# A decoder layer in one kernel: weight stream, recurrent steps, dense expert blocks and last sums rearranged

## Chip, cores and metric

One core of a Trainium2 chip. The metric is the device time of one execution in microseconds (us). Engines: TensorE (PE), VectorE (DVE), ScalarE (ACT), GpSimd (POOL), SyncE (SP, which issues most DMAs). All times below come from the measured runs or from one profiled execution.

## What is computed

One layer for a prompt of 512 tokens and 8 single sampled tokens, all in float32, width 1024 (520 columns together, since activations lie transposed):

```python
sh1, sc1, g1, sh2, sc2, g2 = split(silu(c) @ w_ada + b_ada, 6)
h = rms_norm(x, norm1_w) * (1 + sc1) + sh1
qa, ka, va, qh, fh, ih, gh, ga, gb = split(h @ w_in)
att = merged attention of 3 dilated windows, 8 heads (samples: over caches)
f = lb + (1 - lb) * sigmoid(fh)        # recurrent branch, 8 heads, 128 x 128 state
o = chunked recurrence with decay f, key 1 - f, value ih, query silu(qh)
hg = rms_norm(o, hg_norm_w) * silu(gh)
x = x + g1 * ((sigmoid(ga) * (att @ w_br_a) + sigmoid(gb) * (hg @ w_br_b)) @ w_o)
h2 = rms_norm(x, norm2_w) * (1 + sc2) + sh2
x = x + g2 * peer_ffn(h2)              # 16 of 16384 experts for each of 8 heads and token
```

`peer_ffn` chooses experts by two sets of 128 keys, and sums gelu(h2 . u) * weight * v over the chosen rows u, v of two tables of 16384 x 1024.

## The kernel before

Each float32 weight tile (128 x 1024, 512 KB, `raw`) is split into a high part (ACT, `whi`, line 132) and a low part (DVE or POOL, `wlo`, line 133), and each product is three matmuls. `raw` has 4 buffers, `whi` and `wlo` 3.

Stages in order of time:
- Front (to 59 us). `mods` multiplies 8 slabs of `w_ada` as they are (two loads each), `norms` the prompt's norm, then `modulate_chunk` and `modulate_samples` write `hT_hi` and `hT_lo`. This part is put in order by the compiler's planner.
- From line 311 to 919 a section with an order written by hand (`manual_schedule`): each engine, SP's queue too, runs its instructions in the order of the text. `plan` lists the weight tiles; `weights_in` (line 339) hands out tile k, having issued loads to k + 3 and splits to k + 2; `product` multiplies it with `hT`.
- Attention (59 to about 530 us): four pairs of heads, each with 9 products (`qkv`). `beside()` runs one step of each open generator ahead of every product: `second_norms`, and `slots`, the attention of the pair before. `slab` multiplies one of the other 16 slabs of `w_ada` (two short tiles); there is one behind each of the first 16 products.
- Recurrent stage (about 530 to 952 us): for each head four products (f, q, v, gg) and a gate. `chain(h)` (line 709) is a generator of ten steps; two heads are open at a time, and a step of each stands ahead of every product. By step: logarithm of f and its running sum `bb` (scan); `kd`, `eb`, decays 0 and 1; transposes of v (`pts`, `vt`), product k q; transposes of kd, pairs 0 and 1, load of the samples' state `ss`; pairs 2; pairs 3; pairs 4 and 5, update of `ss`; pairs 6, new states; output products and `norm_bc`; the rest of the norm (`finish`) and the gate. `decode_attention` is the samples' attention over the caches in 51 steps: POOL multiplies loaded taps, DVE reduces them, and PE sums (`total`, line 665). `step_all` calls it once after each `beside()`, twice in every fourth step.
- Branches, `w_o`, second norm (952 to 1108 us), then the expert queries and their scores (to about 1213 us). The splits `a_hi`, `a_lo`, `g_hi`, `g_lo` of the two branch inputs stand at the start.
- Choices (about 1224 to 1570 us, again ordered by hand from line 975): `choose_tile` picks 16 of 256 sums for one of four tiles of tokens on DVE, in 16 steps. Tile 3 goes by gathers of single rows (`step`, POOL's indirect DMAs and DVE), tiles 0 to 2 dense: for each of 128 blocks of 128 experts all activations are computed (`dense`, line 1091) and weighted by a matrix G, which is built in 48 steps from one-hot products (line 1356), staged by ACT and written to DRAM (`d_G`). `ahead` computes the dense activations of one of the first NSP = 56 blocks early and stores them (`d_ge`): in choose_tile(3) and choose_tile(0) at every third step with POOL's low split, then with DVE's in the 12 of 16 steps that `GU` names, and what is left after the steps.
- Last stage (1614 to 2437 us): for each block `out_block` adds 18 products with v to six PSUM banks; for blocks from NSP on `dense` is computed here, for the others `ge` is loaded again. The gathers go on beside this.
- Tail: the six banks times `g2b` on DVE, plus x on POOL, stored by SP (lines 1524 to 1531), ordered by the planner.

## Time and profile before

| | us |
|---|---|
| median of 3 runs | 2453.06 (2452.21 to 2458.89) |
| the profiled execution | 2453.66 |
| its span, first to last instruction | 2451.9 |

| engine | busy us | share of the span |
|---|---|---|
| PE | 2297.9 | 94% |
| DVE | 1760.3 | 72% |
| ACT | 1155.0 | 47% |
| POOL | 660.6 | 27% |

The profile gives the busy time of each engine, the TensorE clock that was granted (1.00 is the upper of its two levels), and for each instruction how long its engine stood idle before it and which event ended that. In a row of a stage the five busy times are those of PE, its weight loads, DVE, ACT and POOL. A row in order of time is: start, length, engine, line, operation, output<-inputs, shapes, count, and in brackets the idle time before it and what ended that. DMA moved 495 MB, 202 GB/s on the mean. A wait that the profile puts down to "issue" has no event that it shows.

### The profile page before, as it was taken

How to read it: one execution, taken by the hardware profiler on the slowest of the kernel's cores; microseconds unless marked ns; L12 is line 12 of the kernel's file. 1: busy time of each engine (PE TensorE's matmuls, PEld its weight loads, DVE VectorE, ACT ScalarE, POOL GpSimd, SP SyncE). 2: the span in 40 equal slices, each digit the busy share in tenths (PEclk: the TensorE clock that was granted, in tenths of full speed). 3: DMA queues.
4: the chain of work that ended last, by engine and by line, in shares of the span. 5: the costliest groups of instructions: out<-in, count | busy, mean ns of one | idle time of the engine just before them, and what ended most of it. 6: DMA issues, size and time to landing. Idle time of an engine off the chain costs nothing.

```text
span 2451.9 us, 37852 instructions
## 1 busy us (share of the span) xinstructions
PE 2297.9 (94%) x14547; PEld 2118.4 (86%) x14547; DVE 1760.3 (72%) x3156; ACT 1155.0 (47%) x1850; POOL 660.6 (27%) x450
## 2 busy tenths in 40 slices
PE   6899999999888988999978989999999999999997
PEld 3788999989888888989978989988888888888886
DVE  3677566548766665547998897477888878788876
ACT  3556566445444443243337778633333333333332
POOL 1110121102221223004450001034444445454433
PEclk9998999999899999999998999989999999999999
DMA  6453212234442324423344555779999999999996
GB/s 220 155 167 113 81 55 70 64 121 141 138 140 90 115 97 157 157 94 96 96 135 168 195 209 199 265 275 331 343 351 328 365 323 344 345 348 331 347 309 206
DMA packets 197466, 495.49 MB, mean 202 GB/s; under 512 B 18123, under 2 KB 84651, under 8 KB 195749
## 3 DMA queue, kind: packets, MB, share of 16 engines
q1 hardware_dynamic: 147636, 313.02, 38.0%
q0 software_dynamic: 39456, 143.28, 16.3%
q10 hardware_dynamic: 10192, 36.77, 4.0%
q8 instruction: 114, 1.87, 0.3%
q14 instruction: 68, 0.55, 0.1%
HBM read 439.17 MB, written 54.49 MB: 201 GB/s over the span
## 4 chain that ended last, share of the span: by engine, by line
PE 43%; DVE 7%; ACT 3%; DMA 1%; issue 1%; ACTq 0%; POOL 0%; POOLq 0%; DVEq 0%; SPq 0%
PE acc L1471 21%; PE ph L1091 16%; PE pp L180 3%; PE pp L1356 2%; ACT oa L1348 1%; DVE wlo L133 1%; ACT whi L132 1%; DVE e L1151 1%; ACT stage L1363 1%; DVE y L1121 1%; DVE sel L1153 0%; PE pt L1177 0%; DMA vr<-in_peer_v 0%; DVE oa L1342 0%; DVE e L1148 0%
## 5 line engine op out<-in xcount | busy, mean ns | idle before, releaser
L133 DVE TENSOR_TENSOR wlo<-raw,whi 128x1024 fp32r<-128x1024 f32 (+1 forms) x254 | 320.0, 1265 | 176.4 <-ACT whi L132 175.2
L1245 POOL DMA_INDIRECT gat<-in_peer_u,idx x128 | 212.6, 1661 | 628.1 <-DVE junk L1272 442.2
L1091 PE MATMUL ph<-h_hi,whi 128*128 128x384 f32 x1024 | 356.4, 348 | 13.4 <-ACT whi L132 13.4
L1091 PE MATMUL ph<-h_hi,wlo 128*128 128x384 f32 x1024 | 351.8, 344 | 8.4 <-POOL wlo L133 7.3
L1091 PE MATMUL ph<-h_lo,whi 128*128 128x384 f32 x1024 | 350.7, 342 | 0.0
L132 ACT ACTIVATE whi<-raw 128x1024 fp32r<-128x1024 f32 (+1 forms) x284 | 292.8, 1036 | 111.3 <-PE pp L180 58.9
L180 PE MATMUL pp<-hT_hi,whi 128*128 128x260 f32 x1344 | 287.9, 297 | 17.2 <-ACT whi L132 17.1
L180 PE MATMUL pp<-hT_hi,wlo 128*128 128x260 f32 x1344 | 280.0, 291 | 5.1 <-DVE wlo L133 5.1
L180 PE MATMUL pp<-hT_lo,whi 128*128 128x260 f32 x1344 | 279.7, 291 | 0.0
L180 PEld LDWEIGHTS pp<-hT_hi,whi 128*128 128x128 f32 x1344 | 218.7, 199 | 20.3 <-ACT whi L132 18.6
L180 PEld LDWEIGHTS pp<-hT_hi,wlo 128*128 128x128 f32 x1344 | 216.6, 197 | 6.9 <-DVE wlo L133 6.9
L180 PEld LDWEIGHTS pp<-hT_lo,whi 128*128 128x128 f32 x1344 | 217.5, 198 | 0.0
L1091 PEld LDWEIGHTS ph<-h_hi,whi 128*128 128x128 f32 x1024 | 197.4, 193 | 17.8 <-ACT whi L132 14.9
L1091 PEld LDWEIGHTS ph<-h_hi,wlo 128*128 128x128 f32 x1024 | 197.0, 192 | 10.4 <-POOL wlo L133 7.9
L1091 PEld LDWEIGHTS ph<-h_lo,whi 128*128 128x128 f32 x1024 | 197.1, 192 | 2.8
L1471 PE MATMUL acc<-vhi,chi 128*128 128x512 f32 x768 | 195.8, 390 | 0.0
L1471 PE MATMUL acc<-vhi,clo 128*128 128x512 f32 x768 | 195.0, 389 | 0.0
L1471 PE MATMUL acc<-vlo,chi 128*128 128x512 f32 x768 | 194.9, 389 | 0.0
L133 DVE TENSOR_TENSOR vlo<-vr,vhi 128x1024 fp32r<-128x1024 f32 x128 | 156.3, 1221 | 52.7 <-ACT vhi L132 52.7
L132 ACT ACTIVATE vhi<-vr 128x1024 fp32r<-128x1024 f32 x128 | 135.3, 1057 | 114.6 <-PE acc L1471 114.6
L1095 ACT ACTIVATE ge<-ph 128x384 f32<-128x384 f32 x128 | 62.6, 489 | 264.9 <-PE ph L1091 264.5
L1245 POOL DMA_INDIRECT gat<-in_peer_v,idx x128 | 162.7, 1271 | 70.9 <-issue 34.0
(378 smaller groups left out, 4531.9 us busy)
## 6 DMA issues: line engine op xcount, KB each, us to landing
raw<-in_uT SPq DMA_DIRECT2D x128, 512.0 KB
vr<-in_peer_v SPq DMA_DIRECT2D x128, 512.0 KB
raw<-in_w_in SPq DMA_DIRECT2D x84, 512.0 KB
raw<-in_w_ada SPq DMA_DIRECT2D x48, 512.0 KB
d_G<-stage ACTq DMA_DIRECT2D x12, 2048.0 KB
gt<-d_G SPq DMA_DIRECT2D x32, 768.0 KB
d_ge<-ge ACTq DMA_DIRECT2D x56, 192.0 KB
ge<-d_ge SPq DMA_DIRECT2D x56, 192.0 KB
```

What stands on the lines that cost most here:

```text
L132: act.activation(hi, src, AF.Copy)
L133: return (eng or dve).tensor_tensor(out=lo, in0=src, in1=hi.bitcast(F32), op=ALU.subtract)
L180: pe.matmul(ps[:, s, :NH], w[:, k, :], x[:, k, s * NH:(s + 1) * NH], start=first and n == 0, stop=last and n == 2)
L1091: pe.matmul(ph[:, :NB], w[:, k], x[:, k, :NB], start=k == 0 and n == 0, stop=k == KC - 1 and n == 2)
L1095: act.activation(ge, ph[:, :NB], AF.Gelu_apprx_tanh)
L1121: dve.match_replace(out=y[:n], in_to_replace=vals[:, 0:8], in_values=x, imm_value=-3.0e38)
L1151: dve.tensor_tensor(out=e3[:n], in0=e3[:n], in1=pb[:n, :, None, :].to_broadcast([n, H, 16, 16]), op=ALU.mult)
L1245: pool.indirect_dma_start(out=t, out_offset=None, in_=A[tab][0], in_offset=bass.IndirectOffsetOnAxis(ap=idx, axis=0))
L1348: act.activation(oas[g][:, j], oas[g][:, j], AF.Copy, scale=sels[t][:, 0, n + j:n + j + 1])
L1356: pe.matmul(pgs[g // 2][:, g % 2, j * P:(j + 1) * P], oa[:, j], ob[:, j], start=True, stop=True)
L1363: act.activation(st[:, :, n0:n0 + 8], pgs.pop(b).rearrange("p s (n i) -> p i (s n)", i=P), AF.Copy)
L1471: pe.matmul(acc[2 * t + d], a[:, t * P:(t + 1) * P], b[:, d * 512:(d + 1) * 512], start=first and n == 0, stop=last and n == 2)
```

## The change

The functions for the plan of tiles move ahead of the front, and `weights_in` is divided into `fetch` and itself; `fetch(0)` is called in the front behind the third slab's columns. The 16 slabs stand behind every other product of the first 32. In `chain`, the scan moves one step later, the transposes of v from the third to the fourth step (in front of the pairs) with kd's behind the pairs, the broadcast load `vb` a step later, and the update of `ss` from the seventh step to the end of the eighth. `finish` runs its matmuls and its square root and returns the other two instructions, which `product` runs after the next tile's loads and splits. The samples' attention gets two calls in every third step. `a_lo` is split on DVE alone. NSP is 60: `ahead` is called in every second step of the two choices, and in 11 of 16 steps of the G loop. In the tail DVE makes three of the six additions, and three of the stores go out by ACT's queue.

```diff
-NSP = 56
+NSP = 60
-GU = (0, 1, 2, 4, 5, 6, 8, 9, 10, 12, 13, 14)
+GU = (0, 1, 3, 4, 6, 7, 9, 10, 12, 13, 15)
 ...
+    def with_slab(hp, n):
+        return (9 * hp + n) % 2 == 0 and 9 * hp + n < 32
 ...
-            if hp == 0 or hp == 1 and n < 7:
-                plan += slab_plan(8 + 9 * hp + n)
+            if with_slab(hp, n):
+                plan += slab_plan(8 + (9 * hp + n) // 2)
 ...
+    def fetch(k):
+        while at_[0] < min(len(plan), k + 4):
+            src, kc = plan[at_[0]]
+            parts[at_[0]] = wtile("raw", F32, RAW)
+            dma.dma_start(parts[at_[0]].rearrange("p (k c) -> p k c", k=kc), src)
+            at_[0] += 1
+        while at_[1] < min(len(plan), k + 3):
+            hi, lo = wtile("whi", F32R, 3), wtile("wlo", F32R, 3)
+            split(hi, lo, parts[at_[1]])
 ...
         for s in mods((0, 4, 1, 5, 2, 6, 3, 7), st, small):
             if s == 0:
                 norms()
+            if s == 1:
+                fetch(0)
 ...
     def product():
-        return proj(None, KC, hT_hi, hT_lo, None, weights_in())
+        w = weights_in()
+        end()
+        return proj(None, KC, hT_hi, hT_lo, None, w)
 ...
             act.activation(two(rs), half(ps), AF.Sqrt, bias=eps)
-            dve.reciprocal(rs, rs)
-            dve.scalar_tensor_tensor(out=x, in0=x, scalar=w, in1=rs, op0=ALU.mult, op1=ALU.mult)
+            def rest():
+                dve.reciprocal(rs, rs)
+                dve.scalar_tensor_tensor(out=x, in0=x, scalar=w, in1=rs, op0=ALU.mult, op1=ALU.mult)
+            return rest
 ...
             bb = t2("bb")
+            yield
             dve.tensor_tensor_scan(bb, reset, lf, 0.0, op0=ALU.mult, op1=ALU.add)
-            yield
 ...
-            pts = bank("pts")
-            pe.transpose(out=pts[:NS, :P], in_=v[:, NT:], identity=ident)
-            vs = hp_.tile([NS, P], F32, tag="vs", name="vs")
-            act.activation(vs, pts[:NS, :P], AF.Copy)
-            after(lambda: dma2.dma_start(d_hv[h], vs))
-            vt = rows(v, "vt")
 ...
             yield
-            kt = rows(kd, "kt")
+            pts = bank("pts")
+            pe.transpose(out=pts[:NS, :P], in_=v[:, NT:], identity=ident)
+            vs = hp_.tile([NS, P], F32, tag="vs", name="vs")
+            act.activation(vs, pts[:NS, :P], AF.Copy)
+            after(lambda: dma2.dma_start(d_hv[h], vs))
+            vt = rows(v, "vt")
             placed = [pairs(0), pairs(1)]
             sides(2)
             decays(3)
             for x in placed:
                 x()
+            kt = rows(kd, "kt")
 ...
             neighbours()
-            for b in range(NS):
-                dve.scalar_tensor_tensor(out=ss[:, b], in0=vb[:, b], scalar=k[:, NT + b:NT + b + 1], in1=ss[:, b],
-                                         op0=ALU.mult, op1=ALU.add)
 ...
                 states.append(new)
+            for b in range(NS):
+                dve.scalar_tensor_tensor(out=ss[:, b], in0=vb[:, b], scalar=k[:, NT + b:NT + b + 1], in1=ss[:, b],
+                                         op0=ALU.mult, op1=ALU.add)
 ...
-            finish()
-            dve.tensor_mul(hg[:, h], ob, d["gg"])
+            rest = finish()
+            def gated():
+                rest()
+                dve.tensor_mul(hg[:, h], ob, d["gg"])
+            ends.append(gated)
 ...
-            for _ in range(2 if late_steps[0] % 4 == 0 else 1):
+            for _ in range(2 if late_steps[0] % 3 == 0 else 1):
 ...
-        split(a_hi[:, c], a_lo[:, c], att[:, c], pool if c % 2 else dve)
+        split(a_hi[:, c], a_lo[:, c], att[:, c], dve)
 ...
     for k, _ in enumerate(choose_tile(3, sel3)):
-        if k % 3 == 0:
+        if k % 2 == 0:
             ahead(pool)
 ...
     for k, _ in enumerate(choose_tile(0, sel)):
-        if k % 3 == 0:
+        if k % 2 == 0:
             ahead(pool)
 ...
             dve.tensor_mul(y, acc[2 * t + d], g2b[:, cols_])
-            pool.tensor_tensor(out=y, in0=y, in1=xo[t][:, cols_], op=ALU.add)
-            dma.dma_start(O["y_prompt"][t][:, cols_], y)
+            ys.append((y, xo[t][:, cols_], O["y_prompt"][t][:, cols_]))
+    for i in (5, 0, 4, 1, 3, 2):
+        y, x, out = ys[i]
+        (dve if i > 2 else pool).tensor_tensor(out=y, in0=y, in1=x, op=ALU.add)
+        (dma if i > 2 else nc.scalar).dma_start(out, y)
```

## Rows read from the trace of the kernel before

**Rows 1.** Stages: from:to, length, busy us (instructions), granted clock, DMA share, GB/s.

```profile
0.00:59.20 59.20, 39.53 (x177) 18.65 (x177) 20.44 (x48) 19.39 (x36) 6.71 (x13) 0.92 0.63 220
59.20:350.00 290.80, 278.75 (x2025) 249.54 (x2026) 202.38 (x274) 176.01 (x245) 39.50 (x27) 0.96 0.36 118
...
500.00:960.00 460.00, 405.27 (x3140) 394.73 (x3140) 299.73 (x545) 221.51 (x347) 93.83 (x67) 0.92 0.39 128
...
1190.00:1290.40 100.40, 82.61 (x499) 80.86 (x497) 95.13 (x348) 34.47 (x45) 54.14 (x25) 0.94 0.43 130
1290.40:1570.20 279.80, 260.22 (x1667) 256.43 (x1668) 228.55 (x457) 223.52 (x518) 14.63 (x10) 0.96 0.57 196
1570.20:1613.60 43.40, 35.47 (x167) 33.81 (x167) 11.59 (x12) 12.93 (x17) 0.00 (x0) 0.84 0.67 238
1613.60:2436.80 823.20, 819.91 (x3986) 728.32 (x3984) 667.20 (x852) 299.19 (x401) 376.11 (x259) 1.00 0.94 332
2436.80:2451.90 15.10, 1.90 (x5) 0.28 (x4) 6.78 (x7) 1.17 (x2) 9.16 (x6) 0.67 0.42 150
```

**Rows 2.** Front: instructions in order of time, a stretch, sizes of loads.

```profile
59.18 0.80 PE L180 MATMUL pp<-hT_hi,whi 128*128 128x260 f32 x2 [14.51 <-ACT whi L132]
...
48.51 1.24 DVE L133 TENSOR_TENSOR hT_lo<-hs,hT_hi 128x64 fp32r<-128x64 f32 x1
...
50.73 0.43 SPq L347 DMA_DIRECT2D raw<-in_w_in  x1
...
15.00:20.00 5.00, 5.00 (x22) 3.51 (x21) 0.00 (x0) 3.47 (x6) 0.00 (x0) 1.00 1.03 411
...
raw<-in_w_in SPq DMA_DIRECT2D x84, 512.0 KB
```

**Rows 3.** Who ended PE's waits from 500 to 960: total, times, longest.

```profile
PE pts L783 <- ACT v L434: 26.4, 7, 5.4
PE pp L180 <- ACT a_hi L132: 7.7, 1, 7.7
PE pl L761 <- DVE w L740: 7.4, 8, 1.9
PE ptm L788 <- issue: 5.6, 1, 5.6
PE pl L761 <- DVE w L746: 3.6, 3, 2.7
```

**Rows 4.** One head's start in order of time, ACT and DVE.

```profile
664.22 0.63 ACT L721 ACTIVATE kd<-kd 128x512 f32<-128x512 f32 x1 [7.42 <-DVE kd L720]
...
667.26 0.58 ACT L434 ACTIVATE v<-pp 128x520 f32<-128x520 f32 x1
...
653.96 1.22 DVE L715 TENSOR_TENSOR_SCAN bb<-reset,lf 128x512 f32<-128x512 bf16 x1 [4.31 <-ACT lf L713]
...
660.31 2.17 DVE L836 SCALAR_TENSOR_TENSOR ss<-vb,k,ss 128x128 f32<-128x128 f32 x8
```

**Rows 5.** A dense block in the chain that ended last; size of a reload.

```profile
1622.02 4.21 PE ph L1091 x24
...
ge<-d_ge SPq DMA_DIRECT2D x56, 192.0 KB
```

**Rows 6.** Who ended PE's waits from 1290.4 to 1570.2.

```profile
PE pp L1356 <- ACT oa L1348: 18.7, 14, 3.0
```

**Rows 7.** First choices in order of time, POOL and DVE.

```profile
1238.68 9.85 POOL L133 TENSOR_TENSOR wlo<-raw,whi 128x1024 fp32r<-128x1024 f32 x3 [7.73 <-ACT whi L132]
...
1246.19 2.42 DVE L1141 TENSOR_SCALAR pp<-pos 128x128 uint32<-128x128 uint32 x1
1248.53 0.21 DVE L1142 TENSOR_SCALAR pp<-pos 128x128 uint32<-128x128 uint32 x1
```

**Rows 8.** Samples' attention in order of time: POOL's addition, PE's sum.

```profile
912.77 1.28 POOL L674 TENSOR_TENSOR tap<-tap 67x512 f32<-67x512 f32 x1
...
925.58 1.00 PE L665 MATMUL pav<-one_v,tap 128*128 128x1 f32 x8
```

More of the change, by code (lines that the diff above doesn't have):

```diff
@@ L241, in layer, with wcol, acol, hcol @@
     hT_lo = fp.tile([P, KC, N], F32R, name="hT_lo")
+    def wcol(c0):
+        return A["w_in"][c0 // P]
+    def acol(t, g, hp):
+        return wcol(t * 1536 + g * 512 + hp * P)
+    def hcol(i, h):
+        return wcol(4608 + i * D + h * P)
+    def gcol(i):
+        return wcol(8704 + i % 2 * D + i // 2 * P)
+    FIRST = ((0, 0), (1, 0), (0, 1), (1, 1), (0, 2), (1, 2), (2, 0), (2, 1), (2, 2))
+    plan = []
+    def with_slab(hp, n):
+        return (9 * hp + n) % 2 == 0 and 9 * hp + n < 32
+    def slab_plan(s):
+        return [(A["w_ada"][s, k2], 4) for k2 in (1, 0)]
+    for hp in range(4):
+        for n, (t, g) in enumerate(FIRST):
+            plan.append((acol(t, g, hp), KC))
+            if with_slab(hp, n):
+                plan += slab_plan(8 + (9 * hp + n) // 2)
+    plan += [(hcol(i, 0), KC) for i in (1, 0, 2, 3)] + [(gcol(i), KC) for i in range(G0)]
+    for h in range(8):
+        plan += [(hcol(i, h + 1), KC) for i in (1, 0, 2, 3)] if h < 7 else []
+        plan += [(gcol(i), KC) for i in GT[h]]
+    parts, at_ = {}, [0, 0, 0]
+    def fetch(k):
[7 more added lines that the diff above has]
+            split(hi, lo, parts[at_[1]])
+            parts[at_[1]] = [x.rearrange("p (k c) -> p k c", k=plan[at_[1]][1]) for x in (hi, lo)]
+            at_[1] += 1
+    def weights_in():
+        k = at_[2]
+        at_[2] += 1
+        fetch(k)
+        return parts.pop(k)
     with tc.tile_pool(name="st", bufs=1) as st:
@@ L312, in layer, with end @@
     flow.__enter__()
-    def acol(t, g, hp):
-        return wcol(t * 1536 + g * 512 + hp * P)
-    def hcol(i, h):
-        return wcol(4608 + i * D + h * P)
-    def gcol(i):
-        return wcol(8704 + i % 2 * D + i // 2 * P)
-    FIRST = ((0, 0), (1, 0), (0, 1), (1, 1), (0, 2), (1, 2), (2, 0), (2, 1), (2, 2))
-    plan = []
-    def slab_plan(s):
-        return [(A["w_ada"][s, k2], 4) for k2 in (1, 0)]
-    for hp in range(4):
-        for n, (t, g) in enumerate(FIRST):
-            plan.append((acol(t, g, hp), KC))
-            if hp == 0 or hp == 1 and n < 7:
-                plan += slab_plan(8 + 9 * hp + n)
-    plan += [(hcol(i, 0), KC) for i in (1, 0, 2, 3)] + [(gcol(i), KC) for i in range(G0)]
-    for h in range(8):
-        plan += [(hcol(i, h + 1), KC) for i in (1, 0, 2, 3)] if h < 7 else []
-        plan += [(gcol(i), KC) for i in GT[h]]
-    parts, at_ = {}, [0, 0, 0]
-    def weights_in():
-        k = at_[2]
-        at_[2] += 1
-        while at_[0] < min(len(plan), k + 4):
-            src, kc = plan[at_[0]]
-            parts[at_[0]] = wtile("raw", F32, RAW)
-            dma.dma_start(parts[at_[0]].rearrange("p (k c) -> p k c", k=kc), src)
-            at_[0] += 1
-        while at_[1] < min(len(plan), k + 3):
-            hi, lo = wtile("whi", F32R, 3), wtile("wlo", F32R, 3)
-            split(hi, lo, parts[at_[1]])
-            parts[at_[1]] = [x.rearrange("p (k c) -> p k c", k=plan[at_[1]][1]) for x in (hi, lo)]
-            at_[1] += 1
-        return parts.pop(k)
+    ends = []
+    def end():
+        while ends:
+            ends.pop(0)()
     def product():
-        return proj(None, KC, hT_hi, hT_lo, None, weights_in())
+        w = weights_in()
+        end()
+        return proj(None, KC, hT_hi, hT_lo, None, w)
     late = []
@@ L566, in second_norms @@
             for n in range(6):
[L567 removed]
+                norms_.pop((hp, n))()()
                 yield
@@ L589, in layer @@
                     under = None
-                if hp == 0 or hp == 1 and n < 7:
+                if with_slab(hp, n):
                     under = slab()
@@ L857, in chain @@
                 states.append(new)
+            for b in range(NS):
+                dve.scalar_tensor_tensor(out=ss[:, b], in0=vb[:, b], scalar=k[:, NT + b:NT + b + 1], in1=ss[:, b],
+                                         op0=ALU.mult, op1=ALU.add)
+            after(lambda: dma2.dma_start(O["hgrn_s"][h], ss))
             after(lambda: dma2.dma_start(O["hgrn_p"][h], states[3]))
@@ L898, in layer @@
             step_all()
+            end()
         begin()
@@ L1524, in layer @@
     xo = [x_rows(d_x[t], P) for t in range(3)]
+    ys = []
     for t in range(3):
```

6 lines of the change are left out of this document (1 added, 5 removed).

## Prediction

> **What bounds the kernel now.** I read the table of stages first: busy time of each engine, granted TensorE clock and DMA share in stretches cut where the work changes. TensorE (PE) is busy in 820 of 823 us of the last stage, 279 of 291 in the attention, and idle for 54.7 us of the recurrent stage, 17.8 of the first choices, 19.6 beside the one-hot products, 7.9 in the stretch after them, 19.7 in the front and 13.2 in the tail [rows 1]. No other engine is full in any stage but VectorE (DVE) with 95 of 100 us in the first choices [rows 1]. So PE sets the time, its instructions are the same after the change, and a gain can come from two places only: PE's idle time, 148 us in the eight rows together, and the time that it works at the lower of its clock levels. The granted clock is a mean of 1.2 and 2.4 GHz; 0.92 over 460 us of the recurrent stage is 0.08 x 460 x 2 = 74 us at the lower level, 0.84 over 43.4 us after the one-hots is 14 us, and it follows the idle stretches (1.00 in the last stage, which has hardly any) [rows 1]. Then I read who ended PE's waits in each stage, and then single waits in order of time.
>
> **Front.** PE stands for 14.51 us until 59.18, for the first part of the first weight tile; that tile's load was issued at 50.73, because it comes behind the front in the order. The last operand of the product, the samples' low part of hT, is done at 48.51 + 1.24 = 49.75 [rows 2]. With four loads issued and three tiles split at the third slab, PE waits for hT instead, and starts 59.18 - 49.75 = 9.4 us earlier. The low clock after the pause, which now partly runs out while PE stands, moves behind the restart; I take off 1.4 for it: -8. The cost that could show: the four loads are 2.1 MB, 5.1 us at the 411 GB/s of 15 to 20 us, a stretch in which DMA is already full [rows 2]. If SP sends them ahead of the last slabs' loads, those come up to 5 us late. The splits add 3 ACT and 3 DVE instructions of about 1.1 and 1.2 us in a part where DVE is busy 20 of 59 us [rows 1]; if the planner, which orders this part, puts them among the last modulations, they cost up to their sum on DVE, 3.7. Bounds -2 and -11.
>
> **Slabs and attention.** The 16 slabs, now behind the first 16 products, go behind every other one of 32. PE's work and DMA bytes are equal. PE is idle for 12.0 us in the 291 us of this stage [rows 1], nearly all of it in the first nine products, where a slab's two short parts leave too little time to split the next tile and no attention steps stand between. Nine such places become five: -12.0 x 4/9 is -5; some comes back where slabs now meet attention steps: -3.5, bounds 0 and -6.
>
> **Recurrent steps.** Here lies most of the gain. Waits of PE in this stage: 26.4 us in 7 places for the copy of v (transposes `pts` of a head's third step), 7.4 and 3.6 for decay products of DVE, 5.6 at the stage's start, 7.7 at its end [rows 3], which leaves 4.0 of the 54.7 in small ones. One wait read in time: ACT's copy of v, at 667.26, is behind the exponentials of kd, and those waited 7.42 us for DVE's kd; DVE had itself stood 4.31 us for ACT's logarithm at the scan and then spent 2.17 us on the state updates of the samples before it came to kd [rows 4]. The change touches each link: the scan goes one step later (no stop of DVE), the state updates go behind the new states, and the transposes of v one step later, a whole product after v. So the 26.4 go. The 3.6 and about 5 of the 7.4, which come behind the reciprocal and the state updates, go with the delayed `rest`. What stays: 5.6 + 4.0 + 2.4. What is late next: first, the products with the samples' states one step after the updates, which now come after DVE's new states; by the one head that I followed, PE arrives about 1 us early. Second, five PSUM tiles in one step where three were, out of four banks, so the fifth waits for ACT's copy of the one before, another 1 us. That is 8 x 2 = 16 us of new waits. The queues that the moved instructions pass: SP's store and broadcast load of v go one step later and are read one step later too; DVE's work in a head is the same. Waits fall from 47.0 to about 28: -19. The low clock: of 74 us I expect 16 fewer while PE works, at half speed: -8. Term -27. Bounds: all waits and half of the low clock gone but the 5.6 and 4.0, -42; every removed wait formed again but a fifth, -8.
>
> **Attention of the samples, branches.** Two calls in every third step instead of every fourth: of 52 calls needed, 41 steps gave 51, now 39 steps give 52, so the sums are done two steps before the end and a_hi can be split before the last gate. The 7.7 us for a_hi [rows 3] shrink, but the last head's norm still ends last for the second product: -5, bounds 0 and -8. Moving two a_lo splits from POOL to DVE is hidden there.
>
> **Four more blocks beside the choices.** One dense block is 24 products in 4.21 us, and leaves the last stage: 4 x 4.21 = -16.8 there [rows 5]. The moves: 8 instead of 6 blocks in each of the two first choices, 33 instead of 36 among the one-hots, 8 instead of 5 after them.
> First choices: DVE sets their length, PE has 17.8 us of idle time and gets 16.8 us of work. About 13 fit, the rest delays nothing since the stage ends with DVE. Cost 0, with 4 us either way.
> Beside the one-hots: PE loses 3 x 4.21 = 12.6 us. Its waits there, 18.7 us in 14 places for ACT's weighing [rows 6], come in steps without a block; these are now 15 instead of 12, so 3 x 18.7/14 = 4 comes back: -8.6.
> After them: 12.6 us more, into 7.9 us of PE's idle time [rows 1] of which about half is filled, and 14 us of low clock of which 6 go at half price: +12.6 - 4 - 3 = +5.6.
> Last stage: its DMA share is 0.94 at 332 GB/s, 273 MB [rows 1]. Four weight tiles (512 KB) become reloads of 192 KB [rows 2, 5], so 272 MB go in 806 us: 337 GB/s. I take +1 for that.
> Sum 0 - 8.6 + 5.6 - 16.8 + 1 = -18.8; bounds +2 (DVE slowed by POOL's splits, DMA holding the last stage) and -26.
> POOL makes the splits of the first choices. Three of them took 9.85 us beside DVE's wide products, and a DVE instruction on 128 x 128 elements took 2.42 us, the next of its kind 0.21 [rows 7]. The Trainium skill's GPSIMD Engine Reference (Specifications) says that the two engines share their SBUF interfaces and contend when DVE reads two tensors from SBUF; the trace agrees. By that rule alone each added split could cost DVE 2.2 us, an estimate of 8.8 for four, and the sum would be -10 in place of -18.8. I stay at 0 because only every second of these calls falls into the wide products, as before.
>
> **Tail.** POOL's six additions fill 9.2 of the last 15.1 us [rows 1]; three of them take half, and DVE gets three more behind its own work: -2, bounds +1 and -4.
>
> **Sum.** -8 - 3.5 - 27 - 5 - 18.8 - 2 = -64. The profiled execution took 2453.66 (span 2451.9), the median of three runs is 2453.06, so the same difference applies: 2389.
>
> **Rivals.**
> B: the waits of the recurrent steps form again, at the samples' states and the banks, at some 5 us per head; the term there is -4 in place of -27, so 2412. For it: DVE is busy 300 of 460 us there and serial with ACT; against: its stops for the logarithm are gone.
> C: DMA becomes the bound of the last stage. If 332 GB/s is what it can move, 272 MB take 819 us instead of 806, and the time is 2402. For it: share 0.94; against: PE waits for nothing there, and 411 GB/s ran in the front [rows 2]. The Trainium skill's page DMA: Bandwidth & Descriptors (Specifications) gives about 358 GB/s of HBM as a core's limit; by it the margin is 6%, by the 411, which differ from it, 18%.
> D: the change does not do what it says in the front: the planner leaves loads or splits behind the modulations. The term is 0, so 2397.
> E, slower: the quicker calls of the samples' attention. PE's sums over the taps wait in PE's order for POOL's additions, and all products stand behind them. POOL ended one at 914.05, PE read it at 925.58, 11.5 us later [rows 8]. Steps get shorter and double calls more frequent; if the margin turns negative, PE stands. At 10 us for each of the eight sums this is +80: -64 + 80 = +16, so 2469. It decides from a tap that lands more than 11 us later relative to PE's step. Against: POOL is busy 94 of 460 us [rows 1].
>
> **How the numbers follow.** Forecast 2389 (own range 2364 to 2410) 0.62, B 0.17, C 0.11, D 0.06, E 0.04. Leaving out E, the upper part of B and the ends of the forecast gives 2355 to 2424 for eight in ten. A measurement of this kernel can tell 0.3%, 7 us, from no change. All cases but E lie below 2446: faster 0.94; same 0.02 (many bounds at their poor ends together); slower 0.04.
>
> **What would show it.** Right: PE's first weight product near 50; no wait at the transposes of v; idle time of the recurrent stage near 30 and its clock near 0.95; 4 fewer blocks in the last stage, which is near 806 us and still without PE waits. Wrong: new waits at the samples' states or the taps' sums; ACT's splits in the last stage waiting for loads; first choices longer than 104 us.

## The result and the profile after

The changed kernel takes 2412.11 us (median of four runs, 2408.19 to 2421.14) against 2452.64 beside it: a ratio of 0.9832, 95% interval 0.9809 to 0.9855, well clear of the 0.3% that a measurement can tell. The forecast was 2389, its own range 2364 to 2410, the whole range 2355 to 2424. So the direction and the range held, and over a third of the forecast gain did not come. The sum hides more than it shows: three terms gained more than forecast, and two, both around other work that PE was to be filled with, are far off on the other side.

The profiled execution took 2409.3 us, its span 2407.5. The engines on its page, beside the table of before:

```profile
PE 2287.8 (95%) x14547; PEld 2109.0 (88%) x14547; DVE 1764.6 (73%) x3157; ACT 1154.5 (48%) x1850; POOL 653.4 (27%) x449
```

To find where the time went, I cut both spans at the same eight events: first product with a streamed weight tile, first product k q of the recurrent stage, first product with `a_hi`, first and last one-hot product, first and last product of `vhi` and `chi` into the six sums, end. The columns are those of [rows 1]. Before, cut so:

```profile
0.00:59.18 59.18, 39.51 (x177) 18.63 (x177) 20.42 (x48) 19.39 (x36) 6.71 (x13) 0.92 0.63 220
59.18:530.20 471.02, 458.97 (x3353) 413.81 (x3354) 301.21 (x455) 267.03 (x376) 61.58 (x41) 0.97 0.30 98
530.20:959.28 429.08, 374.36 (x2907) 366.38 (x2905) 287.25 (x515) 211.16 (x331) 93.52 (x65) 0.91 0.40 132
959.28:1298.60 339.32, 314.43 (x2319) 307.27 (x2319) 243.90 (x830) 123.00 (x177) 100.02 (x59) 0.96 0.38 120
1298.60:1569.70 271.10, 252.87 (x1637) 249.40 (x1638) 221.94 (x442) 220.67 (x513) 13.31 (x8) 0.97 0.56 193
1569.70:1613.70 44.00, 36.07 (x172) 34.41 (x172) 11.59 (x12) 13.43 (x18) 0.23 (x1) 0.84 0.67 239
1613.70:2433.80 820.10, 816.82 (x3973) 725.99 (x3972) 665.78 (x850) 299.19 (x401) 375.92 (x258) 1.00 0.94 332
2433.80:2451.90 18.10, 4.90 (x18) 2.51 (x16) 8.20 (x9) 1.17 (x2) 9.34 (x6) 0.72 0.51 185
```

The changed kernel, cut at the same events:

```profile
0.00:51.66 51.66, 40.73 (x178) 19.12 (x178) 22.06 (x43) 19.38 (x34) 6.75 (x12) 1.00 0.67 247
51.66:535.30 483.64, 465.85 (x3348) 419.87 (x3348) 300.41 (x459) 266.87 (x377) 61.50 (x42) 0.95 0.31 96
535.30:928.71 393.41, 357.53 (x2912) 352.14 (x2910) 292.71 (x516) 209.04 (x330) 90.04 (x66) 0.95 0.45 144
928.71:1270.00 341.29, 327.51 (x2415) 321.76 (x2415) 247.10 (x833) 129.97 (x186) 103.89 (x61) 0.97 0.40 128
1270.00:1534.70 264.70, 241.63 (x1541) 236.71 (x1542) 215.79 (x435) 215.10 (x505) 10.78 (x7) 0.97 0.53 185
1534.70:1592.40 57.70, 51.01 (x267) 49.20 (x267) 17.63 (x18) 19.45 (x26) 0.94 (x1) 0.94 0.66 238
1592.40:2393.50 801.10, 798.68 (x3877) 707.66 (x3877) 660.50 (x846) 293.49 (x393) 375.82 (x258) 1.00 0.95 339
2393.50:2407.50 14.00, 4.92 (x18) 2.53 (x16) 8.43 (x12) 1.17 (x2) 3.71 (x3) 0.85 0.67 244
```

The difference of each length, beside the term of the prediction:

| stage | forecast us | measured us |
|---|---|---|
| front | -8 | -7.5 |
| slabs and attention | -3.5 | **+12.6** |
| recurrent steps, with the wait for `a_hi` | -27 - 5 | -35.7 (the wait itself: +0.2) |
| branches to first choices | 0 | +2.0 |
| one-hot loop | -8.6 | -6.4 |
| after the loop | +5.6 | **+13.7** |
| last stage | -15.8 | -19.0 |
| tail | -2 | -4.1 |
| sum | -64 | -44.4 |

In the front PE now waits for hT, as forecast (instructions in order of time, the ones that answer to [rows 2]):

```profile
51.37 0.24 ACT L132 ACTIVATE hT_hi<-hs 128x64 fp32r<-128x64 f32 x1
51.64 1.28 DVE L133 TENSOR_TENSOR hT_lo<-hs,hT_hi 128x64 fp32r<-128x64 f32 x1
51.66 0.58 PE L180 MATMUL pp<-hT_hi,whi 128*128 128x260 f32 x1 [3.83 <-ACT hT_hi L132]
```

In the recurrent stage the wait of 26.4 us for v [rows 3] is gone. What ended PE's waits there (total, times, longest):

```profile
PE pc L662 <- DVE sc L656: 9.1, 1, 9.1
PE pl L782 <- DVE w L761: 9.0, 7, 2.2
PE pp L180 <- ACT a_hi L132: 7.9, 1, 7.9
PE pl L779 <- DMA tap<-in_cache_kv_w: 5.2, 1, 5.2
```

The first line is new: 9.1 us in a single place, at the transposes of the samples' scores. The decay products of the second line have not got quicker (L782 here is L761 of before: 9.0 us for 7.4 [rows 3]); those of L746 no longer wait. The last line stands near the stage's start, where 5.6 us stood before. Beside the one-hots the wait for ACT's weighing [rows 6] has grown from 18.7 us in 14 places:

```profile
PE pp L1383 <- ACT oa L1375: 24.0, 20, 3.2
```

### The profile page after: what moved, and what is told of

Same layout as the page of the kernel before. It is cut to its first block, busy times and chain, and to the rows that moved or that the text cites. A ratio compares the mean times of both kernels' runs of the same rounds, so it can differ in the third digit from the quotient of the medians.

```text
span 2407.5 us, 37833 instructions
## 1 busy us (share of the span) xinstructions
PE 2287.8 (95%) x14547; PEld 2109.0 (88%) x14547; DVE 1764.6 (73%) x3157; ACT 1154.5 (48%) x1850; POOL 653.4 (27%) x449
## 4 chain that ended last, share of the span: by engine, by line
PE 42%; DVE 8%; ACT 4%; issue 2%; DMA 1%; ACTq 0%; SPq 0%; POOLq 0%; DVEq 0%
PE acc L1498 21%; PE ph L1118 16%; PE pp L180 3%; PE pp L1383 2%; ACT oa L1375 1%; DMA gt<-d_G 1%; DVE wlo L133 1%; ACT whi L132 1%; DVE e L1178 1%; DVE oa L1369 1%; DVE sel L1180 1%; DVE y L1148 1%; ACT stage L1390 1%; PE pt L1204 0%; DVE e L1175 0%
## 5 line engine op out<-in xcount | busy, mean ns | idle before, releaser
L132 ACT ACTIVATE whi<-raw 128x1024 fp32r<-128x1024 f32 (+1 forms) x284 | 292.8, 1037 | 104.6 <-PE pp L180 60.0
L180 PE MATMUL pp<-hT_hi,whi 128*128 128x260 f32 x1344 | 288.3, 297 | 6.3 <-ACT hT_hi L132 4.9
L180 PE MATMUL pp<-hT_hi,wlo 128*128 128x260 f32 x1344 | 279.7, 291 | 1.6 <-DVE wlo L133 1.6
L180 PE MATMUL pp<-hT_lo,whi 128*128 128x260 f32 x1344 | 280.7, 292 | 0.5 <-DVE hT_lo L133 0.5
L180 PEld LDWEIGHTS pp<-hT_hi,whi 128*128 128x128 f32 x1344 | 218.2, 199 | 8.7 <-ACT hT_hi L132 5.1
L180 PEld LDWEIGHTS pp<-hT_lo,whi 128*128 128x128 f32 x1344 | 218.4, 198 | 0.8 <-DVE hT_lo L133 0.8
L180 PEld LDWEIGHTS pp<-hT_hi,wlo 128*128 128x128 f32 x1344 | 216.6, 197 | 2.2 <-DVE wlo L133 2.2
L132 ACT ACTIVATE vhi<-vr 128x1024 fp32r<-128x1024 f32 x128 | 135.3, 1057 | 113.6 <-PE acc L1498 105.4
L1272 POOL DMA_INDIRECT gat<-in_peer_v,idx x128 | 157.6, 1231 | 75.1 <-issue 35.3
```

Source lines behind the costliest of these rows:

```text
L132: act.activation(hi, src, AF.Copy)
L180: pe.matmul(ps[:, s, :NH], w[:, k, :], x[:, k, s * NH:(s + 1) * NH], start=first and n == 0, stop=last and n == 2)
L1272: pool.indirect_dma_start(out=t, out_offset=None, in_=A[tab][0], in_offset=bass.IndirectOffsetOnAxis(ap=idx, axis=0))
```

## The experiments

Each edit starts from the changed kernel, or where it says so from the kernel before. Lengths of stages come from one profiled execution of each, cut at the events above. A difference of less than 7 us (0.3%) between two medians cannot be told from nothing. A stage's length moves too where nothing in it was edited: the attention took 466.5 to 472.2 us in the four kernels that have its old code and the old front, the recurrent stage 392.5 to 396.5 us in the six that have its new code untouched. A difference of some 5 us in one stage of one execution is therefore a hint and not a result.

**Attention: where the slabs stand.** The stage should have gained 3.5 us and lost 12.6. PE waits there for the low half of a slab's second tile:

```profile
PE pm L421 <- DVE wlo L133: 10.7, 10, 2.0
```

That is 10.7 us in all, in 10 places, 2.0 the longest. (The expectations below say 22.7 for it, which is too much: I had added up the columns.) One of the places in order of time, DVE and PE: a reciprocal of a norm and a product stand on DVE ahead of three splits, and the slab's second half waits for the first of these.

```profile
75.46 3.40 DVE L404 RECIPROCAL rs<-rs 128x520 f32<-128x520 f32 x1 [3.74 <-ACT rs L401]
78.90 0.76 DVE L405 SCALAR_TENSOR_TENSOR x<-x,wq,rs 128x520 f32<-128x520 f32 x1
79.57 4.61 DVE L133 TENSOR_TENSOR wlo<-raw,whi 128x1024 fp32r<-128x1024 f32 x3
...
80.85 0.29 PE L421 MATMUL pm<-wlo,c 128*10 128x256 f32 x1 [2.05 <-DVE wlo L133]
```

That was the theory: VectorE comes late. Three kernels tested it.

```
slabs_first16:  with_slab(hp, n): 9 * hp + n < 16
slabs_on_pool:  split(hi, lo, parts[at_[1]], pool if plan[at_[1]][1] == 4 else dve)
slabs_late16:   with_slab(hp, n): 19 <= 9 * hp + n < 35
```

> The changed kernel (2412.1) with the 16 slabs of the attention back behind the first 16 products; nothing else is undone. Theory (the spread slabs meet attention steps, so that VectorE comes late to the low half of a slab's second tile, which TensorE then waits for, and the clock falls more often): the waits of the slabs' products for wlo at their second part go from about 22.7 us back to about 4, the stage from the first product to the end of the attention goes from 483.6 us to about 470, and the time is 2399, between 2396 and 2403. Rival (the stage grew because the stream of weights starts earlier and the same work now stands ahead of it, or because of the delayed second part of the norms): the stage stays at 480 to 484 us and the time at 2409 to 2415.

Measured: 2397.53 us (ratio to before 0.9767, 0.975 to 0.9784), the time that the theory gave. The stage:

```profile
51.31:525.10 473.79, 458.51 (x3347) 413.73 (x3347) 300.21 (x459) 266.82 (x377) 64.09 (x42) 0.97 0.31 98
```

9.8 us shorter than 483.64. The waits for a slab's low half are 6.3 us here, in 5 places, for 10.7 in 10; the theory had 4. Of the 9.8 us 2.5 are PE's idle time (483.64 - 465.85 = 17.8, here 15.3) and 7.3 busy time, with the same instructions at a mean clock of 0.97 in place of 0.95. So the place of the slabs is the cause, but the larger part of the loss is no wait.

> The changed kernel with its spread slabs, where GpSimd in place of VectorE makes the low halves of the slabs' tiles (32 instructions, about 3.3 us each by the split of the first choices, in a stage in which GpSimd is nearly idle). Theory (VectorE's order is what holds the slabs up): the waits for the slabs' wlo shrink from 22.7 us to under 10, though not to nothing, since GpSimd's split takes longer than VectorE's 1.2 us, and the time is 2400 to 2406. Rival 1 (it is not who splits but that a slab's two short tiles leave no time for the splits behind them): the waits stay near 23 us or grow by 2 us for each slab, and the time is 2412 to 2440. Rival 2 (GpSimd slows VectorE's wide instructions beside it): VectorE's attention instructions get longer by some tenths and the stage by 5 us or more.

Measured: 2410.45 us (0.982, 0.9795 to 0.9844), no different from the changed kernel. The stage, and its waits for slabs:

```profile
56.31:536.60 480.29, 466.52 (x3348) 421.20 (x3348) 264.37 (x429) 266.40 (x377) 127.69 (x72) 0.95 0.31 97
```

```profile
PE pm L421 <- POOL wlo L133: 4.1, 2, 2.1
```

The waits fell from 10.7 to 4.1 us, the stage got 3.3 us shorter, and the clock stayed at 0.95; the first product came 4.7 us later (56.31 for 51.66), which ate the rest. VectorE's lateness is thus about a quarter of the 12.6 us, not the main thing. Rival 2 did not happen: VectorE's other instructions in the stage took 212.9 us together, 212.5 in the changed kernel. GpSimd's split took 2.40 us on the mean of 30, not the 3.3 I had assumed.

> The changed kernel with the same 16 slabs behind products 20 to 35, so that every one of them stands beside attention steps (in the changed kernel 11 of 16, with slabs behind the first 16 products 8). Theory (a slab and an attention step together make a long stretch of short matmuls between two products, after which the clock falls; the DVE wait for wlo is not the main part, since GpSimd's splits took most of it away and the time stayed): although the first products get rid of their slabs, the time at the lower clock in the attention rises from 48 us to 60 or more, the stage takes 486 to 495 us in place of 483.6, and the time is 2415 to 2424. Rival (it is the spreading over every other product that costs, with twice as many turns from tiles of 1024 to pairs of short tiles): dense again as in the kernel before, the stage takes 470 to 478 us and the time is 2399 to 2407.

Measured: 2396.27 us (0.9764, 0.9746 to 0.9782). My theory had moved to "a slab beside an attention step costs", and it fell; the rival stands. All 16 slabs stand beside attention steps here (behind the first 16 products it is 7 of them, not the 8 of the expectation), and the stage is 9.4 us shorter:

```profile
51.60:525.80 474.20, 461.71 (x3348) 416.06 (x3348) 300.08 (x459) 266.96 (x377) 61.70 (x42) 0.96 0.32 98
```

```profile
PE pm L421 <- DVE wlo L133: 10.2, 9, 1.5
```

It even keeps 10.2 us of waits for slabs. What costs is that slabs stand behind every other product: behind consecutive products, early or late, they cost about 10 us less, partly in small waits (12.5 to 15.3 us idle in place of 17.8), partly in the clock. Why the clock falls more often in the alternating order these runs do not settle.

**Recurrent steps.** First the new order alone, in the kernel before:

```
 kernel before + chain(h), rest and end() of the changed kernel
 (slabs, fetch, NSP, calls of decode_attention, tail as before)
```

> The kernel before (2452.6) with only the new order of the recurrent steps: the scan and the transposes of v one step later, the update of the samples' state behind the new states, the second part of the norm behind the next tile's splits. Slabs, start of the stream, blocks, calls of the samples' attention and tail are those of before. Theory (this order alone took the 36 us that the stage lost in the changed kernel): the stage takes 385 to 390 us in place of 422, the time is 2413 to 2420, TensorE's waits for the copy of v are gone, and the 9.1 us wait at the transposes of the scores, which I put down to the quicker calls, is not there. Rival (the earlier start, the slabs or the calls have a share in it): the stage takes 395 us or more and the time is over 2424.

Measured: 2415.08 us (0.9837, 0.982 to 0.9855). The stage up to the product with `a_hi`:

```profile
531.50:920.90 389.40, 363.08 (x2913) 357.79 (x2911) 284.60 (x516) 209.66 (x331) 93.38 (x66) 0.93 0.45 146
```

429.08 became 389.40: -39.7, more than the 35.7 in the changed kernel. Without the wait for `a_hi` that is 381.7, a little under the theory's 385 to 390. The wait at the scores is 2.8 us in 2 places here. So the new order alone gives all of the stage's gain. The changed kernel has 9.6 us more of PE's idle time there (35.9 for 26.3) and 5.6 us less busy time; that the quicker calls of the samples' attention cost the idle time is likely, since the wait at the scores is longer with them, but no run undid them alone, and the 4.0 us in length are no more than such a stage moves by itself.

```
 kernel before: only pts, vs, vt moved behind the step that holds pl and decays(2), kt behind the pairs,
 the load of vb a step later
```

> The kernel before (2452.6) with one move out of the recurrent order: the transposes of v one step later, in the place of kd's, and the load that depends on them a step later; scan, update of the samples' state and norm as before. It tells how much of the 39.7 us (the new order alone took these from the stage) hangs on this wait. Theory (the 26.4 us of waiting for v are the main loss and its copy is late only by that one step): the 26.4 us are gone, the other waits stay as they are, and with their share of the low clock the time is 2420 to 2428. Rival (VectorE's stop at the logarithm and the early update of the samples' state keep ScalarE late, so that TensorE meets the next operand, the decay products, late instead): the waits for v shrink, those at the pairs grow, and the time is 2433 or more.

Measured: 2427.67 us (0.9901, 0.9882 to 0.992), the theory at its upper edge. Stage and waits:

```profile
526.70:933.00 406.30, 370.34 (x2912) 362.52 (x2911) 291.63 (x516) 209.52 (x331) 93.47 (x66) 0.92 0.44 140
```

```profile
PE pl L761 <- DVE w L740: 7.7, 8, 1.4
...
PE pl L761 <- DVE w L746: 3.6, 3, 2.7
PE ptm L786 <- DVE am L773: 3.2, 1, 3.2
```

The 26.4 us are gone and the decay products wait as before (7.7 and 3.6, [rows 3] has 7.4 and 3.6). The stage gained 22.8: 18.8 of PE's idle time, since 7.6 us of waits came up in other places, the 3.2 among them, and only 4.0 of busy time. By the stage alone the time would be near 2430, between theory and rival; the attention, which this edit leaves as it is, was 4.5 us shorter in the profiled execution (466.5 us). This one move is 22.8 of the 39.7; scan, state updates and the delayed norm share the other 16.9, 9.6 of it idle time (36.0 to 26.3) and 7.3 busy time as the clock goes from 0.92 to 0.93.

Then the new wait at the scores. In the changed kernel, in order of time:

```profile
703.75 1.27 DVE L656 TENSOR_REDUCE sc<-pr 128x8 f32<-128x512 f32 x2
...
714.64 0.67 DVE L656 TENSOR_REDUCE sc<-pr 67x8 f32<-67x512 f32 x1
715.37 0.32 PE L662 MATMUL pc<-ident,sc 67*64 67x67 f32 x1 [9.12 <-DVE sc L656]
```

Two sums end at 705.0, the third stands behind a whole step's work on DVE, and PE's transposes are called together with it.

```
         vt = taps(0, 0, 1)
+        yield
         pc = bank("pc")
 ...
         dve.tensor_scalar(s4[:, 1:2], s4[:, 0:1], -1.0, None, op0=ALU.mult)
-        yield
         act.activation(pr, pr, AF.Exp, bias=s4[:, 1:2], accum_out=s4[:, 2:3])
```

> The changed kernel, in which the transposes of the samples' scores stand one call later than the last sum of the scores, and the maximum and the exponentials in one call (the number of calls is the same). Theory (TensorE's 9.1 us wait at these transposes, and some 10 us of low clock around it, come from VectorE's last sum standing behind the whole step's work in the same call): the wait is gone, the stage gets 8 to 12 us shorter, 2400 to 2404. Rival (TensorE was ahead of VectorE by that much anyway and meets the next operand of VectorE instead): a wait of similar length stands at a product of the pairs or at the next transposes, and the time is 2408 to 2414.

Measured: 2397.30 us (0.9764, 0.9738 to 0.979). The wait is gone, no other took its place, and the stage is 380.90 in place of 393.41, -12.5: more than the wait itself.

```profile
534.50:915.40 380.90, 356.72 (x2912) 351.62 (x2910) 289.82 (x515) 208.79 (x330) 90.35 (x66) 0.95 0.47 149
```

```profile
PE pl L782 <- DVE w L761: 4.4, 3, 1.5
```

Little of the surplus is the clock. PE's idle time fell by 11.7 us (35.9 to 24.2), its busy time by 0.8 (357.53 to 356.72): beside the 9.1 us, the decay products wait 4.4 us where they waited 9.0. So the theory is right on the wait, and its low clock gave next to nothing back. Whether the decay products wait less because of this edit is open; in the kernel before with the new order alone they also wait 4.4 us.

**Blocks beside the choices.** Alone, in the kernel before:

```
 kernel before + NSP = 60, GU of 11, "if k % 2 == 0: ahead(pool)" in both first choices
```

> The kernel before with only the four more blocks beside the choices (60 in place of 56, at every second step of the two first choices, at 11 of 16 steps of the one-hots). Theory (the four stages of the changed kernel take up the same differences here): first choices +2, one-hots -6, the stretch after them +14, last stage -19, together -9, so 2441 to 2446. Rival (the +14 comes from the clock or from work that earlier stages pushed there): the stretch grows by 4 to 8 us only, and the time is 2434 to 2439, near the -18.8 of the prediction.

Measured: 2444.30 us (0.995, 0.9932 to 0.9968). First choices +3.1, loop -6.7, after it +11.0, last stage -16.7, together -9.3: the stages take up nearly the same differences without the rest of the change, and the prediction's -18.8 for the blocks did not come. Counting the products of the dense blocks stage by stage (24 each) shows one slip of mine: 15, 36, 7 and 70 blocks before, 19, 32, 11 and 66 after. The last of the loop's 33 blocks stands behind the last one-hot product, so four blocks left the loop and four came behind it, not three.

```
-GU = (0, 1, 3, 4, 6, 7, 9, 10, 12, 13, 15)
+GU = (0, 1, 2, 4, 5, 6, 8, 9, 10, 12, 13, 14)
```

> The changed kernel with 60 blocks, of which 36 stand in the one-hot loop as in the kernel before, so that 5 in place of 8 are left after it. Theory (what the blocks gain in the last stage is given back because moving blocks from the loop to behind it returns too little in the loop, 6.4 of 16.8 us, and costs 13.7 there): loop and the stretch after it take 315 us together, as before the change, in place of 322.4, and the time is 2403 to 2407. Rival (the stretch after the loop is set by the way of G out to memory and back, so that blocks there cost nothing and TensorE would stand instead): the stretch stays above 52 us with a new wait of TensorE of 6 us or more, and the time is 2410 to 2414.

Measured: 2407.63 us (0.9812, 0.9795 to 0.9828); the time stands 0.6 us above the theory's range and 4.5 below the changed kernel, less than the medians can tell; the stages agree with the theory. Loop and stretch after it:

```profile
1271.60:1543.20 271.60, 253.08 (x1639) 249.61 (x1639) 221.69 (x441) 220.70 (x513) 13.40 (x8) 0.97 0.56 193
1543.20:1583.90 40.70, 33.56 (x172) 32.29 (x171) 11.59 (x12) 13.34 (x18) 0.14 (x1) 0.92 0.72 253
```

312.3 in place of 322.4. PE waits 7.1 us for splits in the stretch after the loop, 6.7 in the changed kernel, so no way of G through memory held PE there that would have hidden the blocks.

**The front undone.**

```
-            if s == 1:
-                fetch(0)
```

> The changed kernel without the early start of the weight stream in the front; all else is left. Theory (the early loads and splits bring the first weight product forward by 7.5 us and cost nothing later): the first product starts near 59 in place of 51.7, the stages behind it keep their lengths, and the time is 2418 to 2421. Rival (what the early start wins, the attention loses again, as VectorE and ScalarE are late there by as much): the attention is 5 us shorter than 483.6 and the time is 2410 to 2414.

Measured: 2418.46 us (0.9858, 0.9839 to 0.9878). PE's first product waits as before ("PE pp L180 <- ACT whi L132: 14.6, 1, 14.6") and starts at 59.48; the attention is 2.1 us shorter (481.52). So the early start brings the first product forward by 7.8 us, and perhaps 2 of these are lost in the attention; the whole time is 6.4 us longer without it.

**The wait for the branches.** `att` is complete at 907.9, and yet ScalarE splits it only when the last gate is done:

```profile
927.16 0.70 DVE L900 TENSOR_TENSOR hg<-ob,gg 128x520 f32<-128x520 f32 x1
928.02 2.22 ACT L132 ACTIVATE a_hi<-att 128x520 fp32r<-128x520 f32 x4 [5.13 <-issue]
```

```
 before the last gate's product:
+    for c in range(4):
+        a_hi.append(hb.tile([P, N], F32R, tag="hb", name="a_hi", bufs=8))
+        a_lo.append(hb.tile([P, N], F32R, tag="hb", name="a_lo", bufs=8))
+        split(a_hi[c], a_lo[c], att[:, c])
 (w laid in a tile of vb, pr2 in one of pr, one tile vs in place of two)
```

> The changed kernel (2412.1), in which the parts a_hi and a_lo of the attention's output are made before the last gate's product, in tiles of the pool hb that are free by then (three tiles more there; room for them from sharing three small tiles). Theory (a_hi and a_lo are laid in memory that the recurrent tiles give back only when the last gate's multiplication is done, so that the split, ready since 907.9, waits until 928.0): TensorE's first branch product follows the last head's norm at once instead of 7.9 us later, and is done when the second product's operand comes; the wait at the branches falls from 7.9 to 2 to 4 us and the time by 4 to 5 us, to 2407 to 2409. Rival (ScalarE's order, not the memory, held the split back, or the second product's operand, for which nothing changes, comes later than its start in the changed kernel): the two branch products together start no earlier, and the time stays at 2410 to 2414.

Measured: 2414.78 us (0.9845, 0.9829 to 0.9862): no gain. The wait itself is gone, and the next operand is late in its place:

```profile
918.80 0.51 PE L186 MATMUL pp<-a_hi,whi 128*128 128x260 f32 x2
928.00 0.80 PE L186 MATMUL pp<-g_hi,whi 128*128 128x260 f32 x2 [6.07 <-ACT g_hi L138]
```

From the first recurrent product to the second branch product it is 394.1 us in place of 398.1, no more than this stretch moves by itself, and the time does not show these 4 us; the last stage was 6.7 us longer in the profiled execution, beside one late load of v. So the splits of `att` did not have to wait, whether for memory or for their place in the order, but only the first of two operands depends on it. Which of the two held them, this run does not tell apart, since it moved both.

**Together.**

```
 combined:          slabs_first16 + scores_yield + gu_as_before
 combined_a_early:  the same + a_early
```

> The changed kernel with three of the edits: slabs behind the first 16 products (attention -10 to -13 us), the transposes of the scores one call later (recurrent stage -12.5 us), 36 blocks in the one-hot loop (loop and the stretch after it -10 us). Theory (the three losses stand in different stages and add up): 2412.1 - 33 to 36, so 2376 to 2380. Rival (some of each is given back, as TensorE meets the next late operand or the last stage its DMA sooner): 2384 to 2396.

Measured: 2381.56 us (2377.32 to 2384.94; ratio to before 0.9703, 0.9689 to 0.9717), 30.5 us under the changed kernel. Attention, recurrent stage, loop and stretch after it:

```profile
51.30:523.90 472.60, 459.75 (x3347) 414.00 (x3346) 298.40 (x458) 266.61 (x377) 62.55 (x42) 0.96 0.32 99
523.90:906.80 382.90, 361.33 (x2912) 356.45 (x2910) 289.89 (x515) 208.85 (x330) 93.37 (x66) 0.94 0.46 148
1246.10:1516.40 270.30, 252.09 (x1637) 248.63 (x1638) 222.64 (x444) 220.75 (x513) 13.37 (x8) 0.97 0.56 194
1516.40:1560.20 43.80, 35.96 (x172) 34.31 (x170) 11.58 (x12) 13.39 (x18) 0.18 (x1) 0.84 0.67 238
```

-11.0, -10.5 and -8.3, which add up to -29.8 (alone -9.8, -12.5 and -10.1, together -32.4). The losses do stand in different stages; the sum is a little less here than alone, and the time lies 1.6 us above the theory's range and 2.4 below the rival's. No other of these kernels is faster.

> The kernel of the three edits with a_hi and a_lo made before the last gate's product as well. Theory (the 4.0 us from the first recurrent product to the second branch product that this edit took alone are real, and the 7 us that its profiled execution lost in the last stage, beside one late load of v, are chance): 3 to 5 us under the kernel of the three edits. Rival (the edit also costs in later stages): the same time as the kernel of the three edits or more, with the loss in the last stage again.

Measured: 2382.02 us (0.9701, 0.9687 to 0.9714), the same as without the edit. The rival holds as to the time, though the last stage lost nothing this time (801.5 us); the second branch product comes 389.9 us after the first recurrent product, in the kernel of the three edits 387.7. The edit is worth nothing that these runs can show.

## Why the prediction was right or wrong

- **Front, -8:** right in size (-7.5) and in what PE waits for, with two misses that offset each other. The cost that the prediction named came: SP issues the four loads from 12.83 us on, ahead of those of the last slabs, PE starts its last 16 products with a slab at 43.46 us in place of 40.30, and hT_lo is done at 51.64 + 1.28 = 52.92 in place of 49.75, 3.2 us later. But PE does not wait for this last operand: it starts with hT_hi, at 51.66. For the low clock behind the restart 1.4 us were taken off; with and without the early start the attention differs by 2.1.
- **Slabs and attention, -3.5:** wrong in sign (+12.6), and the one term that broke. The step that failed is "nine such places become five": it counted places where a slab's tiles leave too little time, and took products without a slab for free. Its premise was already off: of the 12.0 us of idle time before, 7.9 stand in the stretch up to 155.4 us, where the tenth slab begins, and not nearly all. Spread, the slabs' own waits rose from 4.0 us in 3 places to 10.7 in 10, and PE's idle time from 12.0 to 17.8. The other 6.9 us are busy time (458.97 to 465.85, clock 0.97 to 0.95), for which the sum had no term at all. With the slabs dense the stage would have come out near the 471.0 of before (473.8 measured), that is no gain either. The bound of 0 at the poor end excluded a loss without a reason in the trace; the sentence "slabs now meet attention steps" named a risk and gave it the wrong sign's room.
- **Recurrent steps, -27:** the main mechanism was right: the 26.4 us for v went, and v_alone shows that they hang on that one step. PE's idle time fell from 54.7 to 35.9, and without the wait for `a_hi` from 47.0 to 28.0, -19.0 where -19 stood in the sum. That it meets the sum is luck: the new waits that I put at 16 us (samples' states and banks) did not form, 9.1 us formed at the scores instead, and the decay products, of whose 7.4 us 5 were to go with the delayed `rest`, wait 9.0, which is 6.6 more than the 2.4 forecast. The term that was mis-sized is the clock: -8 forecast, -16.8 of busy time measured (0.91 to 0.95; 2 x 0.09 x 429 = 77 us at the lower level became 2 x 0.05 x 393 = 39, at half price 19). How much of the low clock goes with a wait I could not have read from the waits: 18.8 us of idle time less came with 4.0 us less busy time in v_alone, 28.4 with 11.3 under the new order alone, 18.8 with 16.8 in the changed kernel. The bound of -42 is no sum of its words either: 37.4 us of waits and half of the 74 us of low clock at half price are 56.
- **Samples' attention, branches, -5:** wrong, +0.2. That the sums are done earlier is so (907.9), but the split of `att` does not follow them at once, and when it is made to, the second product's operand comes 6.07 us late. The premise "the last head's norm still ends last" stood in the prediction; it should have set the term to 0.
- **Blocks, -18.8:** -9.7 measured in the four stages. First choices 0 forecast, +2.0 measured (+3.1 alone), inside the bound of 4, and hardly clear of nothing: the seven other kernels with the same order in that stretch took 339.3 to 341.9 us for it, the kernel before 339.3. The contention that the Trainium skill names (GPSIMD Engine Reference, Specifications) for VectorE instructions with two inputs from SBUF is borne out: a multiplication of two tensors, 128 x 2048, in the choices (L1151, L1178 in the changed kernel) took 3.25 to 3.31 us in three places beside GpSimd's splits and 1.22 to 1.23 in the other five, in either kernel. (The row with 2.42 us in [rows 7] reads one tensor only.) What does not hold is the price per added split, +8.8 for four: in the first choices five instructions of VectorE took longer than their like elsewhere, by 10.6 us together, before the change, and again five, by 10.3, after it. Last stage: -19.0 for -15.8; a block there is worth 4.4 us (307.86 us in 1681 matmuls of before, times 24), not the 4.21 of the one in the chain [rows 5], and the 1 us for DMA was not needed. The loss is around the one-hots: loop and stretch after it were to gain 3.0 and lost 7.3. Taking four blocks from the loop returned 6.4 of 16.8 us. Of the 10.4 us missing, 4.8 are PE's idle time (18.2 to 23.1), as it waits for ACT's weighing in six more places (24.0 us in 20); the other 5.6 are busy time, which fell by 11.2 us only, and why these runs do not settle. Behind the loop the forecast was +5.6 and 13.7 were paid: 4.2 us of the 8.1 between them are the fourth block, and 2.8 are waits that stayed (7.9 us idle before, 6.7 after) instead of being filled by half.
- **Tail, -2:** -4.1, at the bound.
- **Rivals.** 2412 is the number of B, but not by B: its waits did not form again. C is refuted: the last stage took 801.1 us at 339 GB/s, with 2.4 us of PE's idle time. The page of the profile shows slices up to 369 GB/s there; the Trainium skill's DMA: Bandwidth & Descriptors (Specifications) gives about 358 as a core's limit, while its Perfetto Trace Analysis (Roofline) calls that a core's share when two cores use the memory, with more for one alone; the 369 agrees with the second. D is refuted by the front. E did not happen at the taps' sums. A relative of it did, a wait for an operand that another engine makes in the same call, 9.1 us once; that the quicker calls brought it is likely and not shown.
- **Chances.** Three terms beat the forecast, by 14 us together (recurrent order, last stage, tail), and the others missed it by 34, of which attention and the stretch after the loop are 24. The bounds carried the range; the likeliest case's own range missed the time by 2 us.

## What to carry to other kernels

Where work with its own operands is spread between other work, do not take the turns without it for free: behind consecutive products the slabs cost about 10 us less than behind every other one, early or late in the stage, in part by small waits and in part by the clock. An operand that PE reads should be made one call ahead of the call that reads it; moving one `yield` took away a wait of 9.1 us and shortened the stage by 12.5. Filling work pays where the engine that sets the time waits: four blocks taken out of the loop with the waits returned 6.4 us and cost 13.7 behind it. And a sum that comes out right is no proof of its terms; read them one by one.

## What the chip showed that I had not expected

- The clock can fall with hardly a pause of PE. In the changed kernel PE is busy in all but 0.4 us of the 9 us from 148.40, with a slab, an attention step and a norm's sums (matmuls with weights of 10 or 20 columns and short transposes among them), and the end of this stretch runs at the lower level; the next product is back at the upper one. Four stretches, columns as above:

```profile
142.60:148.40 5.80, 5.80 (x51) 5.78 (x50) 2.46 (x4) 2.41 (x4) 0.00 (x0) 1.00 0.52 137
148.40:154.00 5.60, 5.20 (x30) 3.73 (x27) 2.43 (x2) 4.43 (x7) 1.30 (x1) 0.99 0.44 164
154.00:157.40 3.40, 3.40 (x17) 3.13 (x17) 2.23 (x9) 1.76 (x4) 0.00 (x0) 0.51 0.00 0
157.40:162.70 5.30, 5.30 (x46) 5.16 (x45) 4.05 (x4) 2.67 (x3) 0.00 (x0) 1.00 0.55 188
```

- What the clock gives back when waits go is not in proportion to them. In the recurrent stage, at an unchanged number of matmuls, 18.8 us less of idle time came with 16.8 us less busy time in the changed kernel, and with 4.0 us in the kernel where only v's transposes moved; taking the 9.1 us at the scores away brought 0.8.
- GpSimd's subtraction on 128 x 1024 elements took 2.40 us on the mean of 30 in the attention, where three beside VectorE's wide instructions of the first choices had taken 9.85 [rows 7].
